# A further 768 matrix products at the end of a one-core hybrid decoder step

## The chip, the cores and the metric

The kernel runs on one core of one Trainium2 chip. The metric is the device time of an execution in microseconds (us), as the median of the runs. Beside the runs there is one execution that the hardware profiler recorded; its rows give times from the start of its span, which runs from the program's first instruction to its last. TensorE (PE in the rows) multiplies matrices; its weight loads stand in rows of their own (PEld). VectorE is DVE, ScalarE is ACT, GpSimd is POOL, SyncE is SP, and a "q" behind an engine means its queue, which issues DMAs and waits.

## The reference

One inference step with one trunk layer, for a prompt of 1024 tokens and a sample group of 8 sequences with one token each. In short:

```python
xn = rmsnorm(x, norm_mix_w)
sc_b, sc_c, sc_x, z, xbc, dt_raw, q, gates = split(xn @ w_in)
y_a = (sc_b * conv3(sc_c * sc_x)) @ w_sc_out                 # short gated convolution
y_b = group_rmsnorm(ssd(...) * silu(z)) @ w_ssm_out          # Mamba-2 scan, 32 heads
y_c = cross_attention(q, memory) @ w_attn_o                  # 256 memory tokens
x = x + (g_A * y_a + g_B * y_b + g_C * y_c) @ w_merge_o
x = x + (silu(xf @ w_gate) * (xf @ w_up)) @ w_down           # xf = rmsnorm(x, norm_ffn_w)
y = rmsnorm(x, norm_final_w)
```

Everything is float32. Outputs are y for prompt and sample, the memory's keys and values, and the states of the convolutions and of the scan.

## The kernel before

Activations stand transposed: 128 channels on the partitions, 1032 tokens (1024 of the prompt and 8 of the sample) along a row. A float32 operand is split into two float32r parts, "hi" and "lo", and a product of two operands is three matrix products (hi x hi, hi x lo, lo x hi) that add up in PSUM. Each `PE.matmul(out, stationary, moving)` becomes one weight load of up to 128 x 128 and one matmul whose duration depends on the columns of the moving operand.

The work goes through three kinds of products. `gemm` (line 215) takes the 1032 tokens in pieces of 256, 512 and 264 columns, each in a PSUM bank of its own. `st_prod` (line 261) takes half of the tokens in pieces of 256 and 260 columns in two banks, in a scheme of seven products in place of eight. The last stage (lines 2001 to 2018) multiplies the last three blocks of hidden rows into the residual `x2[0]` to `x2[7]`, in four chunks of tokens: 384, 384, 136 and 128 columns. For three output blocks at a time it takes a PSUM tile from `mm_ps`, writes nine products into one bank for each block, and adds the bank to `x2[m]` on VectorE (line 2017).

After each chunk `finish(tiles)` (lines 1979 to 1997) normalises its tokens: TensorE transposes the eight blocks back (line 1987), ScalarE squares and sums (line 1989), VectorE multiplies by the norm's weights (line 1991), a short chain of small instructions makes the inverse root (lines 1994 and 110 to 115), VectorE scales (line 1996), and SyncE issues the DMA to the output (line 1997). The last chunk is that of tokens 768 to 895, and `finish((6,))` is the last thing that the program does; the framework's closing waits and barrier have line 2050.

```python
    def finish(tiles):                                           # 1979
        ...
                PE.transpose(ps[:n, ...], x2[half * 4 + k4][:, ...], ident)      # 1987
        ...
                PE.matmul(pb, wh[:, ks], ah[:, c0:c1], start=(k == 0), stop=False)   # 2013
                PE.matmul(pb, wh[:, ks], al[:, c0:c1], start=False, stop=False)      # 2014
                PE.matmul(pb, wl[:, ks], ah[:, c0:c1], start=False, stop=...)        # 2015
            for m in ms:
                V.tensor_tensor(x2[m][:, c0:c1], ps[:, m - m0, :w], x2[m][:, c0:c1], op=ALU.add)  # 2017
        finish(tiles)                                            # 2018
```

The framework orders each engine's instructions itself: it goes through the program with a list of what is ready, by priority of the source's order, and sets the semaphores. Tiles come from pools by tag: `mm_ps` has two buffers of three banks at the end (tag "mm"), weights have three buffers each for tags "whi" and "wlo" (128 x 1024 float32r). A new tile waits until the last reader of the buffer it takes is done.

Of the kernel before, what the change touches and what calls it, by code (L numbers as in the profile page):

```python
# [10 lines left out]
F32R = mybir.dt.float32r  # L11
# [6 lines left out]
P = 128  # L18
# [28 lines left out]
def tile_kernel(ctx: ExitStack, tc, a, o):  # L47
# [1931 lines left out]
    def finish(tiles):  # L1979
        yts = []  # L1980
        for i in tiles:
            n = P if i < NCK else NS
            yt = ev_tile(f"y{i}", (P, D))
            for half in range(2):
                ps = sm_ps(f"psy{i}{half}")
                for k4 in range(4):
                    PE.transpose(ps[:n, k4 * P : (k4 + 1) * P], x2[half * 4 + k4][:, i * P : i * P + n], ident)  # L1987
                junk = fin.tile([P, 512], F32, tag="fj", name=f"fj{i}{half}")
                S.activation(junk[:n, :], ps[:n, :], AF.Square, accum_out=st[:n, 2 * i + half : 2 * i + half + 1])  # L1989
                c = slice(half * 512, (half + 1) * 512)  # L1990
                V.tensor_mul(yt[:n, c], ps[:n, :], nw[:n, c])
            yts.append((i, n, yt))
        for i, n, yt in yts:
            V.tensor_add(ss[:n, i : i + 1], st[:n, 2 * i : 2 * i + 1], st[:n, 2 * i + 1 : 2 * i + 2])
            rsqrt(fin, rst[:n, i : i + 1], ss[:n, i : i + 1], D, [n, 1], f"f{i}")
            V.tensor_scalar(yt[:n, :], yt[:n, :], rst[:n, i : i + 1], None, op0=ALU.mult)
            SY.dma_start(o["y_p"][0, i * P : (i + 1) * P, :] if i < NCK else o["y_s"][:, 0, :], yt[:n, :])
# [3 lines left out]
    for n3, (c0, c1, tiles) in enumerate(  # L2001
# [15 lines left out]
                V.tensor_tensor(x2[m][:, c0:c1], ps[:, m - m0, :w], x2[m][:, c0:c1], op=ALU.add)  # L2017
        finish(tiles)


# [1 line left out]
_INS = [  # L2022
# [31 lines left out]
```

## Time and profile before

| what | value |
|---|---|
| median of 2 runs | 2485.65 us (2484.97 to 2486.34) |
| profiled execution, its own time | 2481.99 us |
| its span | 2480.1 us |
| mean granted TensorE clock | 0.996 |
| TensorE busy | 2426.3 us, 98% of the span, 18906 matmuls |
| weight loads busy | 2308.0 us, 18906 |
| VectorE, ScalarE, GpSimd busy | 1587.2, 1072.3, 118.3 us |

In the rows of a timeline the first number is the start, the second the duration in us; then engine, line, operation, what it writes and reads, shapes, and how many instructions are merged in the row; in brackets the engine's idle time before it and what ended that. In the rows of a table by stretches, behind the stretch and its length, come the busy time and number of instructions of each engine (TensorE, weight loads, VectorE, ScalarE, GpSimd, or the first two alone where one line was asked for), the granted clock, the share of the DMA engines and GB/s. In the rows of one line's instructions stand the minimum, median and maximum duration in ns, then the first and last start.

### The profile page before, as it was taken

The numbers are of one execution on the slowest core, as the hardware profiler recorded it, in microseconds if no ns is written. First come the engines' busy times: TensorE is split into PE (matmuls) and PEld (weight loads), VectorE is DVE, ScalarE is ACT, GpSimd is POOL, SyncE is SP. The second block draws the span as 40 slices with busy tenths as digits, with TensorE's granted clock in tenths as the row PEclk, the third lists the DMA queues.
The fourth block names the chain that finished last, engine by engine and source line by source line (L and its number), as shares of the span: only waits on it lengthen the run. The fifth ranks groups of instructions, "written<-read, shape, count | busy, mean of one in ns | idle before, by whom it ended". The sixth has DMA issues, their size and how long they took to land.

```text
span 2480.1 us, 45608 instructions
## 1 busy us (share of the span) xinstructions
PE 2426.3 (98%) x18906; PEld 2308.0 (93%) x18906; DVE 1587.2 (64%) x2598; ACT 1072.3 (43%) x1716; POOL 118.3 (5%) x163
## 2 busy tenths in 40 slices
PE   7999999999999999999999989999999999999998
PEld 5899999999999999888888877899999999999998
DVE  5754587777678774656767562454787555476755
ACT  6553455454555535556545441213453333342322
POOL 0200000000000000121120000000000000000000
PEclk9999999999999999999999999999999999999999
DMA  6335334434444456667878677874454323264421
GB/s 199 107 128 171 121 104 154 126 114 120 136 129 140 128 160 205 182 207 262 264 225 286 205 257 236 256 249 154 133 176 145 99 95 112 69 224 144 154 86 69
DMA packets 359661, 404.80 MB, mean 163 GB/s; under 512 B 16422, under 2 KB 286870, under 8 KB 359447
## 3 DMA queue, kind: packets, MB, share of 16 engines
q1 hardware_dynamic: 339006, 344.18, 44.4%
q10 hardware_dynamic: 20449, 57.71, 6.0%
q8 instruction: 148, 2.42, 0.4%
q14 instruction: 58, 0.48, 0.1%
HBM read 286.74 MB, written 115.32 MB: 162 GB/s over the span
## 4 chain that ended last, share of the span: by engine, by line
PE 86%; DMA 6%; DVE 4%; ACT 2%; issue 1%; SPq 0%; ACTq 0%; POOL 0%; DVEq 0%
PE po L215 12%; PE pm L1755 4%; PE ps_q L215 3%; PE pd L215 1%; PE py L998 1%; PE ps_g L215 1%; PE pss L1011 1%; PE po L990 1%; PE Z2m L261 1%; PE C3m L261 1%; PE G18m L261 1%; PE Z14m L261 1%; PE C6m L261 1%; PE G12m L261 1%; PE C4m L261 1%
## 5 line engine op out<-in xcount | busy, mean ns | idle before, releaser
L943 ACT ACTIVATE r<-r,acum 128x128 f32<-128x128 f32 x256 | 79.2, 392 | 4.1 <-DMA r<-ac_d 3.6
L714 DVE SCALAR_TENSOR_TENSOR ax<-u,prm,ax 128x1024 f32<-128x1024 f32 x44 | 56.3, 1280 | 0.1
L975 POOL TENSOR_TENSOR xdd<-xdt,decst 128x512 f32<-128x512 f32 x32 | 38.9, 1215 | 288.8 <-DVE xdt L971 288.8
L884 ACT ACTIVATE st<-st,es 128x128 f32<-128x128 f32 x128 | 41.6, 393 | 22.6 <-DMA st<-in_state_ssm_dram 18.5
L1402 DVE TENSOR_TENSOR yr<-po,yr 128x1032 f32<-128x1032 f32 x8 | 9.8, 1230 | 55.8 <-PE po L215 45.8
L994 DVE TENSOR_TENSOR y<-po,ea 128x512 f32<-128x512 f32 x28 | 19.3, 689 | 37.2 <-PE po L990 37.2
L969 DVE TENSOR_TENSOR r<-r,cbm 128x1024 f32<-128x1024 f32 x32 | 39.2, 1224 | 2.7 <-ACT bT L968 0.5
L886 DVE SCALAR_TENSOR_TENSOR st<-sr,dts,st 128x128 f32<-128x128 f32 x128 | 40.1, 344 | 0.4
L968 ACT COPY bT<-bp 128x128 f32<-128x128 f32 x32 | 8.5, 265 | 69.9 <-DVE cbm L966 69.7
L1989 ACT ACTIVATE fj<-psy 128x512 f32<-128x512 f32 (+1 forms) x18 | 10.7, 595 | 58.9 <-PE psy L1987 58.8
L890 DVE SCALAR_TENSOR_TENSOR sr<-st,sr 128x128 f32<-128x128 f32 x128 | 35.1, 284 | 1.1
L998 PE MATMUL py<-r,xdt 128*64 128x128 f32 x512 | 35.0, 279 | 0.0
L944 ACT ACTIVATE r<-r 128x1024 f32<-128x1024 f32 x32 | 33.8, 1058 | 0.6
L971 DVE TENSOR_TENSOR xdt<-xp,dtT 128x512 f32<-128x512 f32 x32 | 21.9, 685 | 18.6 <-PE xp L964 18.4
L1011 PE MATMUL pss<-xdd,bT 128*128 128x512 f32 x64 | 33.4, 603 | 0.3 <-ACT bT L968 0.3
L1762 DVE TENSOR_TENSOR x<-pm,xT 128x516 f32<-128x516 f32 x16 | 11.1, 695 | 35.1 <-PE pm L1755 35.1
L998 PEld LDWEIGHTS py<-r,xdt 128*64 128x64 f32 x512 | 27.3, 137 | 4.1 <-issue 0.5
L990 PE MATMUL po<-bc,s 128*128 128x128 f32 x224 | 29.8, 276 | 1.0 <-DVE s L1017 1.0
L1024 POOL TENSOR_TENSOR s<-s,cdec 128x512 f32<-128x512 f32 x28 | 30.2, 1078 | 7.4 <-DVE s L1017 7.0
L990 PEld LDWEIGHTS po<-bc,s 128*128 128x128 f32 x224 | 27.6, 191 | 2.8 <-issue 1.6
L1684 DVE TENSOR_TENSOR gt<-po,gt 128x1032 f32<-128x1032 f32 x8 | 9.9, 1232 | 30.0 <-PE po L215 28.2
L717 DVE SCALAR_TENSOR_TENSOR ax<-u,prm,ax 128x1032 f32<-128x1032 f32 x22 | 28.3, 1287 | 0.0
(9065 smaller groups left out, 8992.0 us busy)
## 6 DMA issues: line engine op xcount, KB each, us to landing
r<-ac_d SPq DMA_DIRECT2D x32, 512.0 KB
gt<-gt_d SPq DMA_DIRECT2D x24, 516.0 KB
xs_d<-ax ACTq DMA_DIRECT2D x22, 516.0 KB
gt_d<-G ACTq DMA_DIRECT2D x20, 516.0 KB
x<-xs_d SPq DMA_DIRECT2D x16, 516.0 KB
zs<-zs_d SPq DMA_DIRECT2D x16, 516.0 KB
yb_d<-x SPq DMA_DIRECT2D x16, 516.0 KB
in<-yb_d SPq DMA_DIRECT2D x16, 516.0 KB
```

What stands on the lines that cost most here:

```text
L215: PE.matmul(out[:, c : c + n], wt[:, ks], x[:, c : c + n], start=(k == 0 and i == 0), stop=(k == nk - 1 and i == 2),)
L261: PE.matmul(hv(ps)[:, c : c + n], wt[:, ks], x[:, c : c + n], start=(start and kt == 0 and i == 0), stop=(kt == 3 and i == 2), skip_group_ ...
L714: V.scalar_tensor_tensor(acc[:, :T], u[:, j : j + T], w[j], acc[:, :T], op0=ALU.mult, op1=ALU.add)
L884: S.activation(st[:, i], st[:, i], AF.Copy, scale=es[:, g * 4 + i, b : b + 1])
L886: V.scalar_tensor_tensor(st[:, i], rb, dts[:, g * 4 + i, b : b + 1], st[:, i], op0=ALU.mult, op1=ALU.add)
L943: S.activation(r[:, j, :], r[:, j, :], AF.Relu, scale=-1.0, bias=acum[:, c, h : h + 1])
L969: V.tensor_tensor(r, r, bc(cbm.unsqueeze(1), [P, HPG, P]), op=ALU.mult)
L975: G.tensor_tensor(b3(xdd, HPG), b3(xdt, HPG), bc(decst[:, c, hs].unsqueeze(2), [P, HPG, 64]), op=ALU.mult)
L990: PE.matmul(po[:, t * P : (t + 1) * P], state["s"][:, t * P : (t + 1) * P], bcg[1][:, cs], start=True, stop=True,)
L998: PE.matmul(py[hp : hp + 64, (h // 2) * P : (h // 2 + 1) * P], xdt[:, h * 64 : (h + 1) * 64], r[:, (h % 2) * 4 + h // 2, :], start=True, s ...
L1011: PE.matmul(pss, bT, xdd, start=True, stop=True)
L1755: PE.matmul(hv(ps)[:, c : c + n], wt[:, ks], x[:, half * HT + c : half * HT + c + n], start=(k == 0 and i == 0), stop=(k == KD - 1 and i = ...
```

## The change

Behind the last `finish` the program copies columns 0 to 1023 of `x2[0]` into a float32r tile `mv` (ScalarE) and those of `x2[1]` into `sv` (VectorE), takes a PSUM tile `ps` of three banks, and runs 768 products from them. `sv` gives the stationary 128 x 128 block, from column `t` on; `mv` gives the moving operand, `w` columns from column `m` on; the product goes to the first `w` columns of bank `b`. Each product starts a sum of its own, so it overwrites what stood there, and nothing reads any of the sums. A series is 24 products (the first is twice 24) in which address, width, order and bank follow the functions given.

```diff
         finish(tiles)
 
+    mv, sv = (wp.tile([P, 1024], F32R, tag=t, name=t + "t") for t in ("whi", "wlo"))
+    S.copy(mv, x2[0][:, :1024])
+    V.tensor_copy(sv, x2[1][:, :1024])
+    ps = mm_ps("pt")
+
+    def series(n, mov, stat, width=256, bank=0):
+        for i in range(n):
+            m, t, w, b = (f(i) if callable(f) else f for f in (mov, stat, width, bank))
+            PE.matmul(
+                ps[:, b, :w], sv[:, t : t + P], mv[:, m : m + w], start=True, stop=True, skip_group_check=True
+            )
+
+    def pairwise(n):
+        series(n, lambda i: (i % 2) * 256 + (i // 2 % 2) * 260, lambda i: (i // 2 % 7) * P, lambda i: 256 + 4 * (i % 2), lambda i: i % 2)
+
+    pairwise(48)
+    series(24, lambda i: (i // 6 % 4) * 256, lambda i: (i // 6 * 2 + i % 2) % 8 * P, 256, lambda i: i // 3 % 2)
+    for off in (0, 4, 8, 16, 32, 64, 128):
+        series(24, off, 0)
+    for off in (16, 64):
+        series(24, 0, off)
+    series(24, 0, 0, 256, lambda i: i % 2)
+    for w in (260, 264, 272, 288, 320, 384, 512, 240, 224, 128):
+        series(24, 0, 0, w)
+    series(24, lambda i: (i % 2) * 256, 0)
+    series(24, lambda i: (i % 2) * 520, 0)
+    series(24, lambda i: (i % 2) * 16, 0)
+    series(24, 0, lambda i: (i % 2) * P)
+    series(24, 0, lambda i: (i // 2 % 2) * P)
+    series(24, 0, lambda i: (i % 2) * 144)
+    series(24, lambda i: (i % 2) * 256, 0, lambda i: 256 + 4 * (i % 2), lambda i: i % 2)
+    series(24, lambda i: (i % 2) * 256, 0, lambda i: 256 + 16 * (i % 2), lambda i: i % 2)
+    pairwise(24)
+
```

## The prediction

> **What bounds the kernel now.** I read the head of the page first, then the timeline of the last 30 us, because everything that is added stands at the end of the program, then the queue's own waits, which show what closes the span.
>
> ```profile
> span 2480.1 us, 45608 instructions
> PE 2426.3 (98%) x18906; PEld 2308.0 (93%) x18906; DVE 1587.2 (64%) x2598; ACT 1072.3 (43%) x1716; POOL 118.3 (5%) x163
> PEclk9999999999999999999999999999999999999999
> PE 86%; DMA 6%; DVE 4%; ACT 2%; issue 1%; SPq 0%; ACTq 0%; POOL 0%; DVEq 0%
> ...
> 2468.38 0.67 DVE L2017 TENSOR_TENSOR x<-pl,x 128x128 f32<-128x128 f32 x3
> 2469.69 0.69 DVE L2017 TENSOR_TENSOR x<-pl,x 128x128 f32<-128x128 f32 x3 [0.64 <-PE pl L2015]
> 2471.50 1.07 PE L1987 MATMUL psy<-ident,x 128*128 128x128 f32 x8
> 2471.70 0.49 DVE L2017 TENSOR_TENSOR x<-pl,x 128x128 f32<-128x128 f32 x2 [1.32 <-PE pl L2015]
> 2472.22 0.60 ACT L1989 ACTIVATE fj<-psy 128x512 f32<-128x512 f32 x1 [5.85 <-PE psy L1987]
> 2475.65 0.75 DVE L1996 TENSOR_SCALAR y<-y,frs 128x1024 f32<-128x1024 f32 x1
> 2476.44 0.34 SPq L1997 DMA_DIRECT2D out_y_p_dram<-y  x1
> SPq L2050 <- DMA out_y_p_dram<-y: 2.2, 1, 2.2
> L2050 SPq EVENT_SEMAPHORE  x8: 17/28/28, 2476.8 to 2480.0; - x8
> ```
>
> TensorE is busy for 98% of the span, at full clock in all 40 slices (PEclk), and every matmul has a weight load of its own (18906 of each). The chain is 86% TensorE. So work that is put behind TensorE's last instruction has almost nothing to hide in. What there is to hide in is the end: TensorE's last work, eight transposes, ends at 2471.50 + 1.07 = 2472.57. From there VectorE and ScalarE finish the last 128 tokens until 2476.40, the output DMA is issued at 2476.44, and SyncE waits 2.2 us for it from 2476.9, so until 2479.1. From there the closing barrier runs to 2480.1: 1.0 us. TensorE is therefore idle in the last 7.5 us. That is the cover for the new products.
>
> **What one product costs.** Durations in the rows are latencies of pipelined matmuls, so I take distances between starts. These rows give them for the widths that the change uses:
>
> ```profile
> 399.90 0.41 PE L261 MATMUL X2m<-xnl,X2Th 128*128 128x256 f32 x2
> 402.75 0.40 PE L261 MATMUL X2m<-T42al,X2Dh 128*128 128x256 f32 x2
> 402.99 0.28 PE L261 MATMUL X2m<-T42ah,X2Dl 128*128 128x256 f32 x1
> 1850.00:2250.00 400.00, 397.59 (x3337) 396.35 (x3337) 1.00 0.39 129
> 2420.07 0.34 PE L2015 MATMUL pl<-h19h,wl0l 128*128 128x384 f32 x1
> 2423.03 0.34 PE L2014 MATMUL pl<-h21l,wl0h 128*128 128x384 f32 x1
> 2399.39 0.63 PE L215 MATMUL pd<-h16h,wd162l 128*128 128x256 f32 x3
> 2403.65 0.63 PE L215 MATMUL pd<-h16h,wd164l 128*128 128x256 f32 x3
> 2457.01 0.28 PE L2013 MATMUL pl<-h20h,wl2h 128*128 128x136 f32 x1
> 2458.24 0.28 PE L2015 MATMUL pl<-h21h,wl2l 128*128 128x136 f32 x1
> 2465.02 0.28 PE L2015 MATMUL pl<-h20h,wl0l 128*128 128x128 f32 x1
> 2468.26 0.27 PE L2014 MATMUL pl<-h20l,wl2h 128*128 128x128 f32 x1
> ```
>
> - Pairs of 256 and 260 columns, alternating banks (L261). The first two rows are 12 pairs apart: 2.85 us, 118.75 ns a product. The stretch from 1850 to 2250 us agrees: 397.59 us for 3337 products, 119.1 ns with its few pauses.
> - 384 columns, three in a row into one bank: 17 starts apart, 2.96 us, 174.1 ns.
> - Triples of 256, 512 and 264 columns (L215): nine triples apart, 4.26 us, 473.3 ns a triple.
> - 136 columns: 11 starts apart, 1.23 us, 111.8 ns. 128 columns: 29 starts apart, 3.24 us, 111.7 ns. Eight columns less save nothing: below some width there is a floor at 111.7 ns.
>
> A line through 258 columns (118.75) and 384 (174.1) has 0.4393 ns a column and 5.4 ns over: 256 columns 117.9 ns, 260 119.6, 264 121.4, 272 124.9, 288 131.9, 320 146.0. The triple then leaves 473.3 - 117.9 - 121.4 = 234.0 for 512. At 240 columns the line gives 110.8, so the floor holds there as well.
>
> **The sum over the 768.**
> - 96 products alternate 256 and 260 columns (72 in the two pairwise series, 24 in the third series from the end): 96 x 118.75 = 11.40 us.
> - 24 alternate 256 and 272: 24 x 121.4 = 2.91 us.
> - 408 have 256 columns and vary only in address, order or bank: 408 x 117.9 = 48.10 us.
> - 7 x 24 have 260, 264, 272, 288, 320, 384 and 512 columns: 24 x (119.6 + 121.4 + 124.9 + 131.9 + 146.0 + 174.1 + 234.0) = 24 x 1051.9 = 25.25 us.
> - 72 have 240, 224 and 128 columns, at the floor: 8.04 us.
>
> Together 95.70 us. In the 408 lies the unknown: no row shows products that read the same columns or overwrite the same ones again and again, or whose operands start at 16, 64 or 256 bytes from a round address. The nearest rows on either side are the floor (111.7) and the 256/260 pair plus as much again (118.75 + 7.05), so I bound them at +-7 ns: with 408 + 24 + 96 products, +-3.7 us. I take the line's value, since the row of the pairs has the same weights' width and nearly the same columns.
>
> **The two copies and when the series can start.** They need an operand each, and the new PSUM tile:
>
> ```profile
> L163 ACT CAST wdth<-wdtr x1: 1044/1044/1044, 12.2 to 12.2; 128x1024 fp32r<-128x1024 f32 x1
> 2435.32 0.15 DVE L1994 TENSOR_TENSOR fss<-fst 128x1 f32<-128x1 f32 x1
> 2435.86 0.69 DVE L1991 TENSOR_TENSOR y<-psy,nw 128x512 f32<-128x512 f32 x1 [0.20 <-ACT fj L1989]
> ```
>
> The ScalarE copy costs 1.04 us (L163, same shape) and the VectorE one about 0.75 (L1996, same shape). x2[0] and x2[1] are final in the first L2017 row, by 2469.05. ScalarE idles 5.85 us before 2472.22, so its copy is free. VectorE idles 0.64 and 1.32 us before the next two L2017 rows, so its copy delays them by 0.1 us at most. The two rows at 2435 show that instructions are queued when ready and not in the order of the source: L1994 of one tile runs ahead of L1991 of the next one, which the source has first. So I take both copies as queued before the last tile's finish. The PSUM tile needs the other of two buffers, which the second L2017 row sets free at 2470.38. All three come before TensorE is done with its transposes, so the series follows them without a gap, from 2472.57. Should some products slip in ahead of a transpose, the order changes but TensorE's sum doesn't; the finish then comes later, and it ends with 90 us of cover.
>
> **The end.** TensorE ends at 2472.57 + 95.70 = 2568.27. The last output DMA has landed at 2479.1, so SyncE's waits are over but for TensorE's. Behind it comes the same closing of 1.0 us: span 2569.3, which is 89.2 us more than 2480.1. Nothing is removed, and nothing of before waits for the new products but the barrier. The profiled execution took 1.9 us beside its span (2481.99), 2571.2 after. The median of the runs, 2485.65, lies 3.7 us above the profiled execution; on it the forecast is 2485.65 + 89.2 = 2574.9.
>
> **A rule that gives less.** The Trainium skill, "TensorE: Matmul & The Clock Gate", section "Back-to-back issue gap", has N/2.4 + 2.5 ns as the isolated gap of a matmul at full clock, 109 ns for 256 columns. For the 204,960 columns here that is 87.3 us, 8.4 us less than my sum (an estimate by that page). The rows are against it: 118.75 ns at 258 columns.
>
> **The rivals.**
>
> ```profile
> L102 ACT ACTIVATE root<-ones x1: 203/203/203, 2.1 to 2.1; 128x1 f32<-128x1 f32 x1
> 2474.00:2476.00 2.00, 0.00 (x0) 0.00 (x0) 1.56 (x8) 0.20 (x1) 0.00 (x0) 0.73 0.00 0
> 2476.00:2478.00 2.00, 0.00 (x0) 0.00 (x0) 0.41 (x1) 0.00 (x0) 0.00 (x0) 0.50 0.37 150
> 1474.90:1478.20 3.30, 2.87 (x12) 2.67 (x13) 3.30 (x13) 2.32 (x8) 0.00 (x0) 0.50 0.71 288
> ```
>
> 1. The series starts late. If VectorE's copy stands behind the last finish, it runs from 2476.40 to 2477.15, 4.6 us after TensorE fell idle. By then the granted clock is 0.50 (the row from 2476), and one such phase in mid-kernel lasted 3.3 us and more; at half rate the series loses another 1.7 us. Time: 2574.9 + 4.6 + 1.7 = 2581.2. For it: the source has the copy last. Against: the two rows at 2435. The Trainium skill has the same in "TensorE: Matmul & The Clock Gate", Part 1: half rate after an idle window of about 3.4 us; the rows agree with it.
> 2. The products stream at their columns alone. If the 5.4 ns over the slope are a price of changing operands, which most series don't pay, and the floor too, 204,960 columns x 0.4393 = 90.0 us: 5.7 us less, 2569.2. For it: long repetitions that the kernel never has. Against: every product still loads its weights. The page's formula of above would make it 2566.5.
> 3. Products that overwrite what the one before has just written wait until it is out. One alone shows 0.28 us (the row at 402.99). Some 620 of the 768 stay in one bank: 620 x (0.28 - 0.118) = 100 us more, 2675. Against: the 384-column products write one region three times running at 174.1 ns, though they add to it.
> 4. The other side: not slower. The sums are read by nobody, and if the compiler drops products without a reader, nothing is left but two hidden copies: 2485.65. It decides once fewer than some 480 products stay: TensorE's time then goes below the 49.7 us that are 2%, plus the 6.5 that the idle end hides. Against: L102 writes a tile that nobody reads, and it stands in the trace.
>
> **How the numbers follow.** Forecast 0.72, late start 0.11, bare streaming 0.09, overwrite waits 0.05, dropped products 0.02, the rest unnamed. The time is 2575. The range takes in the forecast with its +-3.7 us, bare streaming down to 2566 and the late start with some of the address cost up to 2584; overwrite waits and dropped products are left out. Two per cent, 49.7 us, is about what a measurement of this kernel tells from no change. Only dropped products give "within", 0.02; I leave 0.01 for faster and 0.97 for slower.
>
> **What would show it.** In the profile after: 19674 matmuls and as many weight loads; TensorE at 0.99 in a block of some 96 us behind the last transposes with VectorE and ScalarE idle; 24 products of one series 2.7 to 2.9 us apart at 256 columns, 5.6 at 512, 2.7 at 240 and below; the chain ending in the new line and not in the output DMA; 1.0 us from TensorE's last product to the end. A gap in front of the block says rival 1, single series far above 118 ns say rival 3 or a cost of addresses. I would be wrong by more than the range only if a whole class of series has another rate than any row of before.

## The result and the profile after

The changed kernel took 2571.2 us (median of 2 runs, 2569.62 to 2572.79), the kernel before 2485.65: a ratio of 1.0357, 95% interval 1.034 to 1.0374. That is 85.5 us more where 89.2 were forecast, and 2571.2 lies in the range of 2566 to 2584. The profiled execution took 2572.79 us, 90.8 more than that of before.

The head of the page after, its clock, the chain that ended last, and the two groups of the new line:

```profile
span 2571.0 us, 47146 instructions
PE 2523.4 (98%) x19674; PEld 2404.1 (94%) x19674; DVE 1587.6 (62%) x2599; ACT 1072.9 (42%) x1717; POOL 118.3 (5%) x163
PEclk9999999999999999999999999999999999999999
PE 87%; DMA 5%; DVE 4%; ACT 2%; issue 1%; SPq 0%; ACTq 0%; DVEq 0%; POOL 0%
L2028 PE MATMUL pt<-whit,wlot 128*128 128x256 f32 (+10 forms) x768 | 96.1, 287 | 0.0
L2028 PEld LDWEIGHTS pt<-whit,wlot 128*128 128x128 f32 x768 | 94.9, 189 | 1.0
```

All 768 products ran (19674 matmuls, 18906 before), each with a weight load, in 96.1 us of busy time with no idle time in front of any. Little else moved: VectorE and ScalarE have one instruction more each and 0.4 and 0.6 us.

The timeline where the block begins:

```profile
2469.90 0.67 DVE L2017 TENSOR_TENSOR x<-pl,x 128x128 f32<-128x128 f32 x3
2470.21 1.05 ACT L2021 CAST whit<-x 128x1024 fp32r<-128x1024 f32 x1 [2.31 <-DVE x L2017]
2470.50 0.67 DVE L2022 CAST wlot<-x 128x1024 fp32r<-128x1024 f32 x1
2471.21 0.69 DVE L2017 TENSOR_TENSOR x<-pl,x 128x128 f32<-128x128 f32 x3
2473.02 1.07 PE L1987 MATMUL psy<-ident,x 128*128 128x128 f32 x8
...
2473.85 6.32 PE L2028 MATMUL pt<-whit,wlot 128*128 128x256 f32 x52
```

Both copies run in the idle time in front of the last additions, and the two L2017 rows stand 1.31 us apart as they did before, so the copies delayed nothing. The first product starts right behind the last transpose. This execution reached its transposes 1.5 us later than that of before (2473.02 and 2471.50), at work that the change doesn't touch; the difference of the two spans, 90.9 us, contains that.

What SyncE waited for at the end, in the same profile:

```profile
SPq L2084 <- PE pt L2028: 89.2, 1, 89.2
SPq L2084 <- DMA out_y_p_dram<-y: 2.2, 1, 2.2
```

The first row is the whole change: after the last output DMA has landed, SyncE waits 89.2 us for the new products. From the last product's start at 2569.63 it is 1.3 us to the end of the span.

The sum, term by term, from the distances between the starts of the 768 records:

| products | forecast us | measured us |
|---|---|---|
| 96 of 256 and 260 columns in turn | 11.40 | 11.34 |
| 24 of 256 and 272 | 2.91 | 2.93 |
| 408 of 256 | 48.10 | 48.51 |
| 168 of 260 to 512 | 25.25 | 25.13 |
| 72 of 240, 224 and 128 | 8.04 | 7.99 |
| all | 95.70 | 95.90 |

Inside the 408 the series differ. Four stretches, each inside one kind: moving offset 0, moving offset 16, 512 columns, and the three narrow widths together (the counts include two or three products that reach in from outside, so the distances below come from the starts):

```profile
2482.50:2485.20 2.70, 2.70 (x25) 2.70 (x24) 0.00 (x0) 0.00 (x0) 0.00 (x0) 1.00 0.00 0
2491.00:2493.60 2.60, 2.60 (x25) 2.60 (x25) 0.00 (x0) 0.00 (x0) 0.00 (x0) 1.00 0.00 0
2530.60:2535.90 5.30, 5.30 (x25) 4.36 (x24) 0.00 (x0) 0.00 (x0) 0.00 (x0) 1.00 0.01 3
2536.10:2543.90 7.80, 7.80 (x73) 7.80 (x71) 0.00 (x0) 0.00 (x0) 0.00 (x0) 1.00 0.00 0
```

From the starts, moving offset 0 took exactly 120 ns a product, offset 4 118.6, 8 116.7, 16 113.3, 32 118.7, 64 119.5; the stationary block shifted by 16 elements 117.8 and by 64 120; banks in turn 120. So between these series addresses are worth up to 6.7 ns a product and the bank nothing.

### The profile page after: what moved, and what is told of

Read it like the earlier page. It is cut to its first block, busy times and chain, and to the rows that moved or that the text cites. A ratio compares the mean times of both kernels' runs of the same rounds, so it can differ in the third digit from the quotient of the medians.

```text
span 2571.0 us, 47146 instructions
## 1 busy us (share of the span) xinstructions
PE 2523.4 (98%) x19674; PEld 2404.1 (94%) x19674; DVE 1587.6 (62%) x2599; ACT 1072.9 (42%) x1717; POOL 118.3 (5%) x163
## 4 chain that ended last, share of the span: by engine, by line
PE 87%; DMA 5%; DVE 4%; ACT 2%; issue 1%; SPq 0%; ACTq 0%; DVEq 0%; POOL 0%
PE po L215 12%; PE pt L2028 4%; PE pm L1755 4%; PE ps_q L215 3%; PE pd L215 1%; PE py L998 1%; PE ps_g L215 1%; PE pss L1011 1%; PE po L990 1%; PE Z2m L261 1%; PE C3m L261 1%; PE G8m L261 1%; PE Z14m L261 1%; PE C6m L261 1%; PE X12m L261 1%
## 5 line engine op out<-in xcount | busy, mean ns | idle before, releaser
L2028 PE MATMUL pt<-whit,wlot 128*128 128x256 f32 (+10 forms) x768 | 96.1, 287 | 0.0
L2028 PEld LDWEIGHTS pt<-whit,wlot 128*128 128x128 f32 x768 | 94.9, 189 | 1.0
```

The costliest lines, as they stand in the source:

```text
L2028: PE.matmul(ps[:, b, :w], sv[:, t : t + P], mv[:, m : m + w], start=True, stop=True, skip_group_check=True)
```

## The experiments

**The sum again.** The changed kernel in more runs, since the medians of two runs and the two profiles stood 5 us apart.

> The changed kernel as it is, in five rounds beside the kernel before on one chip. Theory (block of 95.7 us, of which 6.5 lie in TensorE's idle end): 89.2 us more, a ratio of 1.036. Rival (some 4 us more are hidden or the block is shorter in undisturbed runs, as the medians of two runs each had it): 85.5 us more, a ratio of 1.0344.

2573.44 against 2484.20 us: 89.2 us more, ratio 1.0361 (1.0347 to 1.0375), and 1.0344 lies outside. SyncE's row reads the same in this run:

```profile
SPq L2084 <- PE pt L2028: 89.2, 1, 89.2
```

The 85.5 of the first comparison lies inside the scatter of two medians of two: single executions of the kernel before went from 2481.87 to 2487.61 us in this run.

**Is the idle end a cover?** Everything behind the first series is left out:

```diff
     pairwise(48)
-    series(24, ...)
-    ...
-    pairwise(24)
```

> Only the first series, 48 products, is kept. Theory (TensorE's idle end hides what fits in it): 48 x 118.75 ns = 5.7 us behind the last transposes, so TensorE is done 0.8 us before the last output DMA has landed, and the time is that of the kernel before to within 0.5 us. Rival (whatever is put behind the transposes adds its whole duration, because the copies delay the finish or the end waits for TensorE first): 5.7 us more than before, 0.23%.

Ratio 1.0002 (0.9993 to 1.0011); a full 5.7 us would be 1.0023. The timeline of its end, and behind it SyncE's wait:

```profile
2468.18 1.07 PE L1987 MATMUL psy<-ident,x 128*128 128x128 f32 x8
...
2469.01 5.89 PE L2028 MATMUL pt<-whit,wlot 128*128 128x256 f32 x48
...
2473.13 0.34 SPq L1997 DMA_DIRECT2D out_y_p_dram<-y  x1
```

```profile
SPq L2067 <- DMA out_y_p_dram<-y: 2.1, 1, 2.1
```

The products end at 2474.90, before the output has landed (2.1 us of wait behind 2473.13 + 0.34 and some tenths), and no wait for them appears. The cover is real. To find its edge, the first series stands twice and the rest is left out:

```diff
     pairwise(48)
+    pairwise(48)
```

> The first series twice, 96 products, 11.4 us. Theory (the idle end hides 6.5 us, and what is over that is paid in full): 4.9 us more than before, a ratio of 1.0020. Rival (the first 48 were free because the cover is longer than thought, or because the first products are cheap): 0 to 2 us. Rival (all is paid once the end waits for TensorE): 11.4 us, 1.0046.

Ratio 1.0022 (1.0013 to 1.0032), 5.5 us (3.2 to 7.9), and SyncE's wait is

```profile
SPq L2068 <- PE pt L2028: 4.7, 1, 4.7
```

So 48 products cost nothing, 96 cost 4.7 us, 768 cost 89.2: 11.4 - 4.7 = 6.7 and 95.9 - 89.2 = 6.7 us are hidden, the 6.5 of the forecast and 0.2. (The prediction first calls all 7.5 us of idle time the cover; its sum rightly leaves out the closing of 1.0 us, which comes behind the last wait in any case.)

**The late start.** The stationary operand is copied from the last tile that `finish` scales.

```diff
+            last[:] = [yt]          # in finish, behind its DMA
...
-    V.tensor_copy(sv, x2[1][:, :1024])
+    V.tensor_copy(sv, last[0])
```

> All 768 products, but the stationary operand is copied from the last tile that the finish scales, so the copy can't run before the finish ends (the operand has other values; the products' shapes and addresses stay). Theory: TensorE idles about 4.6 us behind its last transposes, the granted clock falls to 0.50 in that time, and the first products run at half rate for up to 3.4 us: the block of products ends 6.3 us later than in the changed kernel, measured from the last transposes. Rival (the clock doesn't fall in so short a gap, or returns with the first product): 4.6 us later, all products at the distances they have in the changed kernel.

The timeline, and then the stretches from TensorE's idle time on:

```profile
2473.37 1.08 PE L1989 MATMUL psy<-ident,x 128*128 128x128 f32 x8
...
2478.32 0.69 DVE L2025 CAST wlot<-y 128x1024 fp32r<-128x1024 f32 x1
...
2479.16 7.12 PE L2031 MATMUL pt<-whit,wlot 128*128 128x256 f32 x44 [4.71 <-DVE wlot L2025]
```

```profile
2475.70:2479.10 3.40, 0.00 (x0) 0.00 (x0) 2.83 (x9) 0.20 (x1) 0.00 (x0) 0.55 0.00 0
2479.20:2482.40 3.20, 3.20 (x15) 3.20 (x16) 0.00 (x0) 0.00 (x0) 0.00 (x0) 0.50 0.40 160
2482.50:2486.00 3.50, 3.50 (x31) 3.50 (x30) 0.00 (x0) 0.00 (x0) 0.00 (x0) 0.95 0.00 0
```

TensorE idled 4.71 us, the clock stood at 0.50 when the series began, and 15 products in 3.2 us are some 213 ns each. From first to last start the 768 took 97.51 us where the changed kernel's took 95.78: 1.7 us. Together 6.4 us; the runs gave a ratio of 1.0384 (1.037 to 1.0398), where the changed kernel's was 1.0361: 5.7 us. Both parts of the rival's price were right; it only didn't happen in the change. The clock fell before TensorE had idled for the 3.4 us that the prediction names as the idle window: the last transpose ended at 2474.45, and a mean of 0.55 over the 3.40 us from 2475.70 leaves some 0.34 us at full clock, so it fell at about 2476.04, 1.6 us into the idle time.

**What is in a product's 118 ns.** A map of offsets and widths.

```diff
+    for off in range(0, 132, 4): series(24, off, 0)
+    for m0, t0 in ((16, 16), (32, 16), ...): series(24, m0, t0)
+    ...
+    # stationary blocks of 64 and 32 columns: sv[:, :cols], ps[:cols, 0, :w]
```

> Other series of 24 in place of those of the change: moving offset 0 to 128 in steps of 4 elements with the stationary block at 0; nine pairs of offsets; moving offset 144 to 512 in steps of 16; the kernel's pattern (256 and 260 columns, two products a block, alternating banks) at 16 starting offsets; stationary blocks of 64 and 32 columns. Theory (the distance between starts depends on how the moving operand lies to the stationary one): the pairs with equal offsets (16,16), (32,32), (64,64) take 120 ns as (0,0) does, and those with 16 elements between them, (32,16), (48,32), (80,64), (144,128), (272,256), (400,384), take 113.3 ns as (16,0) does. Rival (the moving operand's own address decides): (16,16) takes 113.3 and (32,16) and (32,32) take 118.7. Rival (what stands over the 0.44 ns a column belongs to the load of 128 stationary columns): with 64 and 32 stationary columns 256 moving ones take 113 ns or less at every offset and 128 moving ones 57 to 60; if the load has no part in it, nothing changes with the stationary's width.

(16,16), (32,32) and (64,64) took 119.5 to 119.8 ns, as (0,0) did, and the six pairs with a difference of 16 all 117.8: inside this run what counts is how the two operands lie to each other. Up to offset 124 it repeats after 64 elements, 256 bytes: the sixteen offsets from 0 to 60 and those from 64 to 124 agree within 0.2 ns each, and 28 and 48 are the lowest, at 113.4. Two readings stand against a rule of offsets alone. Offset 16 took 117.9 here and 113.3 in the changed kernel, so the expected 113.3 was a miss. And the six offsets from 176 to 496 that lie 48 beyond a multiple of 64 took 117.8, where 48 and 112 took 113.4. The kernel's pattern of 256 and 260 columns took 116.6 to 120.6 at its sixteen starting offsets. With 64 and 32 stationary columns 128 moving ones took 60.0 to 62.0. At offsets 0 and 16, 256 moving columns took 119.7 and 117.9 ns with 128 stationary ones, 114.3 and 116.6 with 64, and 113.9 and 113.3 with 32: a shorter weight load lowers the distance, so it has a part in the excess.

**Two rates at one address, and the floor.**

```diff
+    for before in (8, 12, 0, 28):
+        series(24, before, 0)
+        series(192, 16, 0)
+    ...
+    for cols in (128, 96, 64, 32):
+        for w in (32, 64, 96, 128, 160, 192, 224, 256, 320, 384, 512): ...
```

> First 192 products at moving offset 16 behind 24 at 8, 12, 0 and 28, and 192 at 28 behind 24 at 24, 0 and 16. Theory (two streams of reads settle into a pattern that depends on what ran before, and keep it): offset 16 takes 113.3 ns behind 8, as in the changed kernel, and 117.8 behind 12, as in the first map, each through all 192; offset 28 likewise may have two values. Rival (the place in the block, or drift): one value for all of a kind, or a change within the 192. Then stationary blocks of 128, 96, 64 and 32 columns with 32 to 512 moving columns, all from offset 0. Theory (the longer of the weight load and the moving stream decides, 111.7 ns for 128 stationary columns, 0.44 ns a moving column and some ns over): below the crossing the distance stays at 111.7, 84 to 88, 56 to 60 and 28 to 32 ns for the four blocks, and at 512 all four are within 8 ns of each other. Rival (the floor is one of issuing an instruction pair): 111.7 for all four.

Stretches of 20 us, each inside a run of 192 products at offset 16, behind 24 at offset 8, 12, 0 and 28:

```profile
2477.00:2497.00 20.00, 20.00 (x172) 20.00 (x171) 0.16 (x1) 0.00 (x0) 0.00 (x0) 1.00 0.07 27
2502.00:2522.00 20.00, 20.00 (x179) 20.00 (x178) 0.00 (x0) 0.00 (x0) 0.00 (x0) 1.00 0.00 1
2527.00:2547.00 20.00, 20.00 (x172) 20.00 (x171) 0.00 (x0) 0.00 (x0) 0.00 (x0) 1.00 0.01 2
2552.00:2572.00 20.00, 20.00 (x172) 20.00 (x171) 0.00 (x0) 0.00 (x0) 0.00 (x0) 1.00 0.00 1
```

172 products in three of them and 179 in one, those that reach in from outside included; by the starts 117.8 and 113.3 ns, and each held through all its 192 products in eight groups of 24. So there are two steady patterns at one and the same address, and the entry chooses. But what ran before doesn't settle which: behind offset 8 it was 113.3 in the changed kernel and 117.8 here, behind 12 it was 117.9 in the map and 113.3 here. What decides stays open. Offset 28 settled at 113.3 each time.

The widths give the floor. Four stretches at 32 moving columns, with 128, 96, 64 and 32 stationary ones:

```profile
2648.00:2650.50 2.50, 2.50 (x26) 2.50 (x24) 0.00 (x0) 0.00 (x0) 0.00 (x0) 1.00 0.00 0
2694.20:2696.10 1.90, 1.90 (x25) 1.90 (x23) 0.00 (x0) 0.00 (x0) 0.00 (x0) 1.00 0.00 0
2725.10:2726.40 1.30, 1.30 (x25) 1.30 (x24) 0.00 (x0) 0.00 (x0) 0.00 (x0) 1.00 0.00 0
2753.00:2753.70 0.70, 0.70 (x24) 0.70 (x23) 0.00 (x0) 0.00 (x0) 0.00 (x0) 1.00 0.00 0
```

By the starts, at 32 moving columns 96, 64 and 32 stationary columns took 85.0, 58.3 and 31.7 ns; 128 took 111.7. That is 5 ns and 0.833 ns a stationary column, so the floor is the weight load. With the load short, 128 and 256 moving columns took 60.2 and 113.3 ns: 0.417 ns a moving column and 6.7 over. That line is no law either: the same short load took 88.6, 103.3, 143.3, 173.3 and 231.7 ns at 192, 224, 320, 384 and 512 moving columns, 2 to 12 ns above it, so some of the excess comes without a long load, and its cause is open. The Trainium skill, "TensorE: Matmul & The Clock Gate", section "LDWEIGHTS (loading the stationary operand)", has columns/1.2 ns; the slope agrees, and the measured loads have 5 ns on top. In the change a product costs the longer of 111.7 and 0.417 w + 6.7 ns, and up to 6.7 more at 256 columns, which goes with the operands' offsets; at 512 columns it costs 8.2 over 220.2.

**Could the kernel use that?** The kernel's own order of products, from shifted tiles.

```diff
+    for kt in range(4):
+        for wt, x, m0 in ((sv, mv, m1), (sv, mv2, m2), (sv2, mv, m1)):
+            for c, n_ in HALF: PE.matmul(...)
```

> The kernel's own order of products (four blocks of rows, for each hi x hi, hi x lo, lo x hi, in pieces of 256 and 260 columns, from four tiles whose bases agree), 48 products for each of 64 pairs of offsets of the two moving tiles, 0 to 112 elements in steps of 16, and of 9 finer pairs. Theory (addresses decide product by product): the pairs differ by up to 5 ns, and some pair near (16,16) takes about 114 to 115 ns a product where the kernel takes 118.75. Rival (the alternation of operands washes it out): all pairs lie between 117 and 120 ns.

> The kernel's order of products again, 48 for each setting: moving operands shifted by 0 to 60 elements in steps of 4, the second stationary tile by 0 to 56 in steps of 8 against the first, with pieces of 256 and 260 columns; then the pieces the other way round, 260 and 256, with shifts of 0 to 48 in steps of 16. Theory (alternation of operands washes the addresses out): most settings between 117 and 120 ns a product, the best of the 192 at 115 to 116. Rival (addresses decide product by product): some settings run the whole pattern at 113.3 ns, which would be worth 4 us per 1000 products in the kernel.

Leaving out the first product of the block, which took 201 ns, all 64 pairs lay between 117.7 and 119.0 ns, and the nine finer ones between 116.7 and 120.1; the 114 to 115 of the theory did not come. Of the 192 settings 189 lay between 117.7 and 121.3 and the best three at 116.9 to 117.1, where 115 to 116 were expected. The rows for the 64 pairs, and for 128 and 64 of the 192:

```profile
2476.40:2839.70 363.30, 363.30 (x3075) 363.30 (x3074) 3.00 (x9) 1.48 (x5) 0.00 (x0) 1.00 0.01 3
```

```profile
2474.70:3205.30 730.60, 730.60 (x6146) 730.60 (x6145) 3.00 (x9) 1.40 (x5) 0.00 (x0) 1.00 0.01 2
3205.40:3571.50 366.10, 366.10 (x3073) 366.10 (x3072) 0.00 (x0) 0.00 (x0) 0.00 (x0) 1.00 0.00 1
```

118.3, 118.9 and 119.2 ns on the mean, where the kernel has 118.75. And the good settings don't repeat: with both moving operands shifted by 4 elements a product took 120.0 in the first of these runs and 117.1 in the second, with a shift of 24 it took 116.7 and 120.2. Alternating operands wash most of the addresses' effect out, and there is nothing here to build a faster kernel on.

**Clock and narrow products.** In the map of widths the clock fell to 0.50 for 23.9 us, 4 us after 128 stationary columns began to meet 32 and 64 moving ones, with TensorE never idle. Tried by itself:

```diff
+    for w in (256, 192, 160, 128, 96, 64, 32, 64, 96, 128, 160, 192, 256):
+        series(300, 0, 0, w)
```

> In place of the series 300 products each at 256, 192, 160, 128, 96, 64, 32, 64, 96, 128, 160, 192 and 256 moving columns, all from one 128-column stationary block and one address. Theory (the clock follows the share of time in which columns stream, and not whether an instruction runs): at 111.7 ns a product the narrow series fall to a granted clock of 0.50 within some 10 us, at 32 and 64 columns for certain and at 192 and 256 not at all, and a product takes 213 ns there; one width between is the border. Rival (the fall in the earlier map was set off by something else in that block, as its switch of series): clock 1.0 and 112 to 120 ns through all widths.

Stretches at 128 columns, at the beginning of 96 and the rest of it, at 32, at 160 on the way up, and at the beginning of 192 and the rest of it:

```profile
2575.95:2609.40 33.45, 33.45 (x302) 33.45 (x302) 0.00 (x0) 0.00 (x0) 0.00 (x0) 1.00 0.01 1
2609.50:2612.50 3.00, 3.00 (x29) 3.00 (x28) 0.00 (x0) 0.00 (x0) 0.00 (x0) 1.00 0.00 0
2612.70:2670.50 57.80, 57.80 (x273) 57.80 (x273) 0.00 (x0) 0.00 (x0) 0.00 (x0) 0.50 0.00 1
2734.50:2798.50 64.00, 64.00 (x301) 64.00 (x302) 0.00 (x0) 0.00 (x0) 0.00 (x0) 0.50 0.00 1
2990.60:3054.50 63.90, 63.90 (x301) 63.90 (x301) 0.00 (x0) 0.00 (x0) 0.00 (x0) 0.50 0.00 1
3054.60:3059.60 5.00, 5.00 (x25) 5.00 (x25) 0.00 (x0) 0.00 (x0) 0.00 (x0) 0.50 0.00 0
3059.80:3090.50 30.70, 30.70 (x277) 30.70 (x277) 0.00 (x0) 0.00 (x0) 0.00 (x0) 1.00 0.01 1
```

At full clock 128 columns a product, in 111.6 ns each, hold it; 96 lose it within 3.2 us. At half clock every product of up to 192 columns takes 213 ns, and 128 and 160 columns, which had held the clock on the way down, don't bring it back; 192 do, after 5.1 us. The theory holds in its direction: the clock fell while TensorE was never idle. In columns a product there are two borders where it had one. In columns a microsecond one may do: 860 (96 in 111.6 ns) lost the clock and 1147 (128) held it, 750 (160 in 213 ns) didn't bring it back and 900 (192) did, so a border between 860 and 900 would fit all four. What the gate counts isn't shown. Its phases at 0.50 lasted 6.83 us in the late start, 23.9 in the map of widths and 447.1 here, which is 2, 7 and 131 times 3.41 us: the clock changes on such a grid, and the 3.2 and 5.1 us are single readings on it. In the change the narrow products are 72, the narrowest 24 at 128 columns, so its clock stayed at full.

## Why the prediction was right

- **What bounds the end.** Right, and shown: the idle end of 6.5 us was a cover of 6.7 (48, 96 and 768 products), and all beyond it is paid.
- **The rate.** Right for reasons that the forecast only half had. The line through two rows, 5.4 ns and 0.4393 a column, is no law: the runs have 6.7 ns and 0.417 a column, the weight load as a floor, and some ns on top, of which a part goes with the operands' offsets and the rest is open. Between 256 and 384 columns, where nearly all products lie, the line comes to the same, presumably because the kernel's rows hold the same excess; no run separates that. The floor of 111.7 would have failed for narrow stationary blocks (31.7 ns with 32 columns).
- **The mis-sized terms.** The 408 products of 256 columns took 0.41 us more than forecast (118.9 ns and not 117.9). The nine series whose offsets are all multiples of 64 elements ran at about 120 and took 0.48 us more, the other eight together 0.06 less. The 512 columns took 228.4 and not 234.0 ns, 0.13 us less. They stay far inside the +-3.7 us that were left for addresses, and the bound of +-7 ns held with room: the steady extremes were 113.3 and 120. The pairwise series ran at 116.7 ns once they were under way, where the kernel's pairs take 118.75. That the whole sum came within 0.2 us is in part luck, since the terms missed in both directions (+0.41 and +0.02 against -0.06, -0.12 and -0.05 us).
- **The start.** Right: both copies were queued into idle time, and the series followed the last transpose without a gap.
- **Late start**, priced at 4.6 + 1.7 us: 4.7 + 1.7 when it was forced.
- **Bare streaming** is wrong at 256 columns even with the smallest weight load (113.3 ns, not 112.5), and the 768 products took 95.9 us where it has 90.0. The 109 ns for 256 columns that the prediction takes from the Trainium skill, "TensorE: Matmul & The Clock Gate", section "Back-to-back issue gap", was seen in no series.
- **Waiting for an overwrite** is refuted: hundreds of products that overwrote the columns of the last one ran at 113 to 120 ns, and in turn between two banks at 120.
- **Dropped products**: all 768 are in the trace.

The time lay 3.8 us under the forecast. Two medians of two runs each have scatter of that size, and in more runs the difference was the 89.2 of the forecast.

## What to carry to other kernels

Appended work costs its own sum less the idle time of its engine before the last output lands; SyncE's last wait reads off what is left. Price a stream of float32r products by the distance between starts in rows of the same stationary width, as the longer of the weight load and the moving stream and some ns on top, and don't tune operand addresses for it while operands alternate. Keep the moving operand at 128 columns or more for 128 stationary ones: at 96 the clock halved here although the engine was never idle.

## What the runs showed that was not expected

- The same series at the same addresses has two steady rates, 113.3 and 117.8 ns, held through 192 products; which one is entered was not settled.
- Inside one run the distance followed the difference of the operands' offsets, up to 124 elements modulo 256 bytes, and neither offset alone; beyond that, and from run to run, the same difference had two rates.
- The clock fell to 0.50 within 3.2 us of busy work at 96 moving columns for 128 stationary ones, and needed 192 columns and 5.1 us to return. The Trainium skill, "TensorE: Matmul & The Clock Gate", Part 1, ties the fall to idle windows; here TensorE was never idle. Streamed columns a microsecond, with one border between 860 and 900, would fit the four readings, but what the gate counts was not settled.
